# Attention in a hybrid block: values as the stationary operand, turned weights of all queries moving, weights divided before they are turned

## The chip, the cores and the metric

The kernel is one program on one core of a Trainium2 chip. The metric is the device time of one execution in microseconds, the median of several runs. TensorE (PE) multiplies matrices; its weight loads are shown as an engine of their own (PEld). VectorE (DVE) and ScalarE (ACT) do elementwise work, GpSimd (POOL) a little, and SyncE (SP) issues most of the transfers. Each engine works through its own queue in order.

## What is computed

Two layers (D 1024, 256 positions, batch 1) of a block: a modulated norm, three branches that mix the positions, and a mixture of experts. The branches are latent attention (8 heads, value width 64), an mLSTM, and dilated attention (8 heads, width 64), which the kernel folds into one masked softmax per head. Cut to what matters:

```
s = einsum('bqhd,bkhd->bhqk', q, k) * scale          # 8 heads, 256 x 256, causal mask
p = softmax(s)                                       # over the keys
o = einsum('bhqk,bkhd->bqhd', p, v)                  # value width 64
ya, yc = o of latent and of dilated attention        # 256 x 512 each
merged = g0*(ya @ w_branch_a) + g1*(yb @ w_branch_b) + g2*(yc @ w_branch_c)
x = x + g_a * (merged @ w_out);  x = x + g_f * moe(norm(x))
```

## The kernel before, in words

All data is fp32. The large products (projections, gates, branch outputs) are made by `dense` and `mm3` (lines 469 to 487): each operand is split into a rounded part and a rest, both of type fp32r, and three matmuls are added up (lines 474, 475, 476). The split of the weights is one ACT copy and one DVE subtraction for each 128x512 piece (line 365), into buffers `rs`, of which four are left for weights. `ul` and `uh` are the split input, read by every projection. DVE also does the products of the modulation (line 284), which have nothing to do with the branches.

`softmax_pv` (line 713) is called four times: for latent attention (called from line 796) and dilated attention (line 954), in each of two layers. It works on 128 queries at a time (t = 0 with 128 keys, t = 1 with 256 keys). For each head TensorE makes the scores (lines 794, 951), DVE adds the mask and takes the row maximum in one operation (line 731), a small DVE operation turns it into the bias (734, 736), and ACT takes the exponential and its row sum `den` (739). Then TensorE turns each 128x128 block of weights P (745), and ACT copies four turned heads at a time from PSUM into T (746). The product with the values (750) has the turned weights of one head as stationary operand (128 keys x 128 queries) and the 64 columns of the values as moving one; queries come out on partitions. DVE then takes the reciprocal of the sums (751) and divides the 128x512 result (752). The result is needed with its features on partitions, so `y_transposed` (756) turns it by eight TensorE transposes of 128x128 (765), and ACT and DVE split it into `yt` (768, 769), the operand of the branch's `dense`. The mLSTM branch uses `y_transposed` too, with a scale (773, 774), and goes on doing so.

An fp32 matmul of the program stands as two records in the trace: line 750 runs 24 times in a call, 96 times in four calls, and has 192 records. Transposes have one record each.

The order of the work on each engine is fixed at compile time by a scheduler that takes what is ready by its own cost model, earlier lines of the program first; so attention and dense products lie interleaved in one queue. Buffers `fs` (nine of 128x2048) are handed out first in, first out (`fs.get`, `fs.put`), so a new user of a buffer waits for its last one. Projections that follow in program order (lines 804, 808, 923, 945, 976) don't need the result of latent attention; the first that does is line 991 with b = 0. Dilated attention's result is needed by line 991 with b = 2.

Of the kernel before, what the change touches and what calls it, by code (L numbers as in the profile page):

```python
# [12 lines left out]
def _warn_once_fixed(msg, *args, **kwargs):  # L13
# [6 lines left out]
F32 = mybir.dt.float32  # L20
F32R = mybir.dt.float32r
I32 = mybir.dt.int32
AF = mybir.ActivationFunctionType
OP = mybir.AluOpType
# [14 lines left out]
C_ID, C_TRI, C_TRIS, C_MLA, C_DIL, C_MLM, C_COS, C_SIN, C_IOTA = (  # L39
    0, 128, 256, 384, 640, 896, 1024, 1088, 1152)  # L40
# [31 lines left out]
def tile_block(ctx: ExitStack, tc: tile.TileContext, x_in, c_in, cst_in, sv_in, aux_in, wada_in, ws_in, out, depth=L):  # L72
    nc = tc.nc
    PE, DVE, ACT, POOL, SP = nc.tensor, nc.vector, nc.scalar, nc.gpsimd, nc.sync
# [8 lines left out]
    def fs_tile(i, dtype=F32):  # L83
        return persist.tile([128, 2048], dtype, name=f"fs{i}")

    fs = Slots([fs_tile(i) for i in range(NB)], fs_tile)

    def xs_tile(i, dtype=F32R):
        return persist.tile([128, 2048], dtype, name=f"xs{i}")
# [4 lines left out]
    xs = Slots([xs_tile(i) for i in range(4)], xs_tile, F32R)  # L94
    rs = Slots([rs_tile(i) for i in range(NR)], rs_tile, F32R)

    def mmt(name="mm"):
        return psum.tile([128, 512], F32, name=name)

    cst = persist.tile([128, N_CST], F32, name="cst")  # L100
# [79 lines left out]
    def cut(h):  # L180
        return A0 if h < 2 else 512
# [81 lines left out]
    for hf in range(2):  # L263
        hs = slice(512 * hf, 512 * hf + 512)
        p = mmt("sm")
# [76 lines left out]
    def layer(l, tail):  # L342
# [185 lines left out]
        else:  # L528
# [21 lines left out]
            for n_, (k0, k1) in enumerate(groups):  # L550
# [11 lines left out]
                p = nxt_p  # L562
# [6 lines left out]
                for j, do in enumerate((first_chunk, second_chunk, third_chunk)):  # L569
# [3 lines left out]
                    n = cut(h_)  # L573
# [68 lines left out]
        for t in range(2):  # L642
            ts = slice(128 * t, 128 * t + 128)
# [10 lines left out]
        va = v_s[:, :1024].rearrange("p (t n) -> p t n", t=2)  # L654
# [18 lines left out]
        scq = work.tile([128, 2, 8], F32, name="scq", bufs=1)  # L673
        for t in range(2):
            ts = slice(128 * t, 128 * t + 128)
# [34 lines left out]
        fs.put(cq_s, up_s, up2_s)  # L710
        pump()

        def softmax_pv(kq, masks, scale, vv, out_s):

            for t in range(2):
                nk = 128 * (t + 1)
                per = 512 // nk
                P_s, T_s = fs.get(), fs.get()
                P = P_s[:, :8 * nk].rearrange("p (h n) -> p h n", h=8)
                T = T_s[:, :8 * nk].rearrange("p (b h n) -> p b h n", b=t + 1, h=8)  # L720
                den = work.tile([128, 8], F32, name="den")
                mx = work.tile([128, 8], F32, name="mx")
                for g in range(8 // per):
                    p = mmt("sm").rearrange("p (h n) -> p h n", h=per)
                    h0 = g % 2 + 4 * (g // 2)
                    hs = slice(h0, h0 + 2 * per - 1, 2)
                    for j in range(per):
                        kq(t, h0 + 2 * j, p[:, j])
                    for j in range(per):
                        h = h0 + 2 * j  # L730
                        DVE.tensor_tensor_reduce(p[:, j], p[:, j], masks[:, 128 * (1 - t):], 1.0, -3.0e38,
                                                 OP.add, OP.max, mx[:, h:h + 1])
                    if scale is None:
                        DVE.tensor_scalar(mx[:, hs], mx[:, hs], -1.0, None, op0=OP.mult)
                    else:
                        DVE.scalar_tensor_tensor(mx[:, hs], mx[:, hs], -1.0, scale[:, t, hs], op0=OP.mult, op1=OP.mult)
                    for j in range(per):
                        h = h0 + 2 * j
                        ACT.activation(P[:, h], p[:, j], AF.Exp, scale=1.0 if scale is None else scale[:, t, h:h + 1], bias=mx[:, h:h + 1],
                                       accum_out=den[:, h:h + 1])  # L740
                for b in range(t + 1):
                    for g in range(2):
                        p = mmt("sm").rearrange("p (h n) -> p h n", h=4)
                        for j in range(4):
                            PE.transpose(p[:, j], P[:, 4 * g + j, 128 * b:128 * b + 128], ident)
                        ACT.activation(T[:, b, 4 * g:4 * g + 4], p, AF.Copy)
                po = mmt("sm").rearrange("p (h d) -> p h d", h=8)
                for h in range(8):
                    for b in range(t + 1):
                        PE.matmul(po[:, h], T[:, b, h], vv[:, b, 64 * h:64 * h + 64], start=b == 0, stop=b == t)  # L750
                DVE.reciprocal(den, den)
                DVE.tensor_tensor(out_s[:, t].rearrange("p (h d) -> p h d", h=8), po,
                                  den[:, :, None].to_broadcast([128, 8, 64]), op=OP.mult)
                fs.put(P_s, T_s)

        def y_transposed(y, scale=None):

            yt_s = xs.get(F32R)
            yt = yt_s.rearrange("p (a b n) -> p a b n", a=2, b=4)
            for bb in range(2):  # L760
                p = mmt("sm").rearrange("p (b n) -> p b n", b=2)
                for b in range(2):
                    for t in range(2):
                        c = (2 * bb + b) * 128
                        PE.transpose(p[:, b, 128 * t:128 * t + 128], y[:, t, c:c + 128], ident)
                if scale is None:
                    s = slice(2 * bb, 2 * bb + 2)
                    ACT.activation(yt[:, 0, s], p, AF.Copy)
                    DVE.tensor_tensor(yt[:, 1, s], p, yt[:, 0, s].bitcast(F32), op=OP.subtract)
                else:  # L770
                    for b in range(2):
                        s = 2 * bb + b
                        ACT.activation(yt[:, 0, s], p[:, b], AF.Copy, scale=scale(s))
                        DVE.scalar_tensor_tensor(yt[:, 1, s], p[:, b], scale(s), yt[:, 0, s].bitcast(F32),
                                                 op0=OP.mult, op1=OP.subtract)
            return yt_s, yt

        qT_s, kT_s = fs.get(), fs.get()
# [2 lines left out]
        for t in range(2):  # L781
            ts = slice(128 * t, 128 * t + 128)
            for src, dst, g in ((qc, qT, V_GQ), (kc, kT, V_GK)):
                for gg in range(2):
                    p = mmt("sm")[:96].rearrange("p (h n) -> p h n", h=4)
# [2 lines left out]
                    o = dst[:, 4 * gg:4 * gg + 4, ts]  # L788
                    ACT.activation(o, p, AF.Copy, scale=sv[:96, g:g + 1])
        fs.put(qc_s, kc_s)  # L790
        ya_s = fs.get()
        ya = ya_s[:, :1024].rearrange("p (t n) -> p t n", t=2)
        def kq_a(t, h, p):
            PE.matmul(p, qT[:, h, 128 * t:128 * t + 128], kT[:, h, :128 * (t + 1)], start=True, stop=True)

        softmax_pv(kq_a, cst[:, C_MLA:C_MLA + 256], scq, va, ya)
        fs.put(qT_s, kT_s, v_s)
        yaT_s, yaT = y_transposed(ya)
        fs.put(ya_s)
        pump()  # L800


# [105 lines left out]
        hg = work.tile([128, 4], F32, name="hg", bufs=1)  # L908
        DVE.tensor_scalar(hg, col(V_HG, 4), 0.5, None, op0=OP.mult)
        ybT_s, ybT = y_transposed(yb, lambda s: hg[:, s:s + 1])  # L910
        fs.put(mo_s)
        pump()


        dn_s, dT_s, dv_s = fs.get(), fs.get(), fs.get()
        dn = dn_s.rearrange("p (a t n) -> p a t n", a=2, t=2)
        dT = dT_s.rearrange("p (a b n) -> p a b n", a=2, b=4)
        dv = dv_s[:, :1024].rearrange("p (t n) -> p t n", t=2)
        yc = dv_s[:, 1024:].rearrange("p (t n) -> p t n", t=2)
        dq8 = work.tile([128, 1], F32, name="dq8", bufs=1)  # L920
        POOL.tensor_scalar(dq8, col(V_DQ), 0.125, None, op0=OP.mult)
        for a in range(2):
# [13 lines left out]
            for bb in range(2):  # L936
                p = mmt("sm").rearrange("p (b n) -> p b n", b=2)
# [11 lines left out]
        def kq_c(t, h, p):  # L949
            r0 = 64 * (h % 2)  # L950
            PE.matmul(p, dT[r0:r0 + 64, 0, h // 2, 128 * t:128 * t + 128], dT[r0:r0 + 64, 1, h // 2, :128 * (t + 1)],
                      start=True, stop=True)

        softmax_pv(kq_c, cst[:, C_DIL:C_DIL + 256], None, dv, yc)
        fs.put(dT_s)
        ycT_s, ycT = y_transposed(yc)
        fs.put(dv_s)
        pump()


# [2 lines left out]
        for b, (yT_s, yT) in enumerate(((yaT_s, yaT), (ybT_s, ybT), (ycT_s, ycT))):  # L963
# [10 lines left out]
            g = g_s.rearrange("p (t n) -> p t n", t=2)  # L974
# [4 lines left out]
            if b == 1:  # L979
# [6 lines left out]
                p = mmt("sm")[:, :160]  # L986
# [21 lines left out]
        for kk, p in transposed(mg):  # L1008
            s = slice(2 * kk, 2 * kk + 2)
# [10 lines left out]
        def small(name, *shape):  # L1020
            return work.tile([128] + list(shape), F32, name=name, bufs=1)
# [219 lines left out]
        ex, d = small("ex", 2, 4), small("d", 2, 4)  # L1241
# [101 lines left out]
    for l in range(depth):  # L1343
        tail = layer(l, tail)
# [130 lines left out]
```

## Time and profile before

| what | value |
|---|---|
| runs, us | 803.78, 804.21, 800.3; median 803.78 |
| profiled execution, own time, us | 806.04 |
| its span from the first to the last instruction, us | 804.3 |
| mean granted TensorE clock | 0.975 of full |
| PE, DVE, ACT busy, share of the span | 95%, 70%, 48% |
| moved by DMA | 234.47 MB, mean 292 GB/s |

The profiled execution lies 2.3 us above the median of the runs. Busy shares are averages over stages with different limits: in the span there are two layers, each with a mixing part (about 20 to 295 us and 412 to 682 us) and an expert part, in which the transfers run near 420 GB/s. A busy TensorE means that a matmul is in its pipeline; how many it gets through is read from the start times of a row and of the row after it.

### The profile page before, as it was taken

The numbers are of one execution on the slowest core, as the hardware profiler recorded it, in microseconds if no ns is written. First come the engines' busy times: TensorE is split into PE (matmuls) and PEld (weight loads), VectorE is DVE, ScalarE is ACT, GpSimd is POOL, SyncE is SP. The second block draws the span as 40 slices with busy tenths as digits, with TensorE's granted clock in tenths as the row PEclk, the third lists the DMA queues.
The fourth block names the chain that finished last, engine by engine and source line by source line (L and its number), as shares of the span: only waits on it lengthen the run. The fifth ranks groups of instructions, "written<-read, shape, count | busy, mean of one in ns | idle before, by whom it ended". The sixth has DMA issues, their size and how long they took to land. (4 is left out here: it accounts for less than half of the span.)

```text
span 804.3 us, 12512 instructions
## 1 busy us (share of the span) xinstructions
PE 760.3 (95%) x4524; PEld 516.8 (64%) x4524; DVE 563.7 (70%) x1414; ACT 386.0 (48%) x851; POOL 30.0 (4%) x58
## 2 busy tenths in 40 slices
PE   4999999999999979999969999999999998999996
PEld 2885887878888854333349588888888876533332
DVE  6889978988899775323379998998757576633234
ACT  6467755664454533111167775576555543512111
POOL 0103000100000010000000400000000001000000
PEclk9999988999999989999989999999999999799999
DMA  8983654788989964999957367778885654499993
GB/s 338 406 343 116 250 211 157 262 309 330 384 302 426 383 247 171 423 421 420 420 211 262 114 253 261 238 262 288 330 326 201 246 202 154 167 420 421 420 422 143
DMA packets 36115, 234.47 MB, mean 292 GB/s; under 512 B 4017, under 2 KB 4689, under 8 KB 10450
## 3 DMA queue, kind: packets, MB, share of 16 engines
q1 hardware_dynamic: 35410, 231.52, 74.5%
q0 software_dynamic: 576, 2.10, 0.8%
q8 instruction: 37, 0.61, 0.3%
q14 instruction: 28, 0.23, 0.1%
q10 hardware_dynamic: 64, 0.02, 0.0%
HBM read 232.55 MB, written 1.06 MB: 290 GB/s over the span
## 5 line engine op out<-in xcount | busy, mean ns | idle before, releaser
L365 ACT ACTIVATE rs<-wa 128x512 fp32r<-128x512 f32 (+1 forms) x224 | 134.9, 633 | 90.1 <-PE mm L475 58.6
L474 PE MATMUL mm<-rs,rs 128*128 128x512 f32 (+1 forms) x432 | 172.1, 401 | 6.2 <-ACT rs L565 5.6
L365 DVE TENSOR_TENSOR rs<-wa,rs 128x512 fp32r<-128x512 f32 (+1 forms) x224 | 148.5, 683 | 39.5 <-ACT rs L365 26.7
L475 PE MATMUL mm<-rs,rs 128*128 128x512 f32 (+1 forms) x432 | 174.2, 404 | 0.4 <-DVE rs L462 0.3
L476 PE MATMUL mm<-rs,rs 128*128 128x512 f32 (+1 forms) x432 | 174.2, 404 | 0.0
L284 DVE SCALAR_TENSOR_TENSOR wa<-wa,cb 128x1024 f32<-128x1024 f32 x90 | 108.0, 1216 | 0.0
L474 PEld LDWEIGHTS mm<-rs,rs 128*128 128x128 f32 x432 | 82.2, 192 | 23.0 <-ACT rs L565 6.9
L475 PEld LDWEIGHTS mm<-rs,rs 128*128 128x128 f32 x432 | 82.7, 191 | 16.6 <-DVE rs L566 1.1
L476 PEld LDWEIGHTS mm<-rs,rs 128*128 128x128 f32 x432 | 83.1, 192 | 15.7 <-issue 1.3
L1210 DVE SCALAR_TENSOR_TENSOR th<-th,mm 128x256 f32<-128x256 f32 x16 | 6.7, 421 | 82.2 <-ACT th L1209 82.2
L1201 PE MATMUL mm<-fs,xs 128*32 128x512 f32 x384 | 58.7, 593 | 0.0
L1201 PE MATMUL mm<-wa,xs 128*32 128x512 f32 x320 | 54.0, 604 | 0.0
L1209 ACT ACTIVATE th<-mm 128x256 f32<-128x256 f32 x16 | 6.1, 383 | 95.8 <-PE mm L1201 95.8
L109 ACT ACTIVATE fs<-fs 128x512 fp32r<-128x512 f32 x32 | 20.1, 629 | 56.3 <-DVE fs L1234 56.3
L1201 PE MATMUL mm<-rs,xs 128*32 128x512 f32 x320 | 42.8, 594 | 0.0
L109 DVE TENSOR_TENSOR fs<-fs,fs 128x512 fp32r<-128x512 f32 x32 | 22.1, 692 | 22.8 <-ACT fs L109 22.8
L474 PE MATMUL mm<-rs,xs 128*128 128x512 f32 x96 | 37.6, 392 | 0.0
L476 PE MATMUL mm<-rs,xs 128*128 128x512 f32 x96 | 37.5, 391 | 0.0
L475 PE MATMUL mm<-rs,xs 128*128 128x512 f32 x96 | 37.4, 390 | 0.0
L1234 DVE TENSOR_TENSOR fs<-mm,fs 128x512 f32<-128x512 f32 x32 | 22.0, 687 | 20.9 <-PE mm L1232 20.9
L365 ACT ACTIVATE rs<-fs 128x512 fp32r<-128x512 f32 x40 | 23.8, 627 | 22.9 <-PE mm L475 14.8
L1201 PEld LDWEIGHTS mm<-fs,xs 128*32 128x32 f32 x384 | 15.9, 110 | 29.0 <-issue 28.4
(333 smaller groups left out, 1276.8 us busy)
## 6 DMA issues: line engine op xcount, KB each, us to landing
wa<-in_ws_dram SPq DMA_DIRECT2D x83, 1024.0 KB, 7.1
fs<-in_ws_dram SPq DMA_DIRECT2D x47, 1024.0 KB, 10.3
wa<-in_wada_dram SPq DMA_DIRECT2D x40, 1024.0 KB, 5.3
rs<-in_ws_dram SPq DMA_DIRECT2D x30, 1024.0 KB, 12.4
wa<-in_wada_dram SPq DMA_DIRECT2D x10, 512.0 KB, 9.9
wa<-in_ws_dram SPq DMA_DIRECT2D x6, 512.0 KB, 9.2
fs<-in_wada_dram SPq DMA_DIRECT2D x6, 512.0 KB, 10.0
fs<-row POOLq DMA_DIRECT2D x4, 512.0 KB, 7.8
```

The source lines that it names most:

```text
L109: return ACT.activation(h, src, AF.Copy), DVE.tensor_tensor(l, src, h.bitcast(F32), op=OP.subtract)
L284: DVE.scalar_tensor_tensor(w, w, 0.5, cb, op0=OP.mult, op1=OP.mult, accum_out=mods[l][:, 2 * i + j:2 * i + j + 1])
L365: pinned(ACT.activation(h[:, cs_], r[:, cs_], AF.Copy), DVE.tensor_tensor(lo[:, cs_], r[:, cs_], h[:, cs_].bitcast(F32), op=OP.subtract))
L474: PE.matmul(o, ah[:, kb + k, ts], hv[:, k], start=st, stop=False)
L475: PE.matmul(o, al[:, kb + k, ts], hv[:, k], start=False, stop=False)
L476: PE.matmul(o, ah[:, kb + k, ts], lv[:, k], start=False, stop=en)
L1201: queued(PE.matmul(pgu[64 * t + 32 * i:64 * t + 32 * i + 32], xg[kb // 2][:, kb % 2, 2 * q + i, t], wv[i][:, k], start=kb == 0, stop=kb == 7))
L1209: ACT.activation(th, pgu[:, :256], AF.Tanh, scale=0.5)
L1210: DVE.scalar_tensor_tensor(th, th, 1.0, pgu[:, :256], op0=OP.add, op1=OP.mult)
L1234: DVE.tensor_tensor(y, py[hf], rows[:, 1, hs], op=OP.mult)
```

## The change

In `softmax_pv` the weights P are divided by their sums before they are turned: for t = 0 by one DVE multiplication of 128x1024, for t = 1 by eight ACT copies of 128x256 with a scale. The reciprocal moves ahead of the turns. The turned weights of both t are kept (T0 for keys 0 to 127, all 256 queries; T1 for keys 128 to 255, the last 128 queries). Then for each head the values (128 keys x 64) are the stationary operand and the turned weights the moving one, 256 columns for T0 and 128 for T1. Two heads write the two halves of the partitions of one PSUM tile. The result has its features on partitions, so that the transposes of `y_transposed` and the division of the result fall away for the two attentions; the split into `yt` stays, now from this PSUM tile. The buffers P0, P1 and T are held from the start of a call to its end; before, two were held for each t, and one for the result.

```diff
-        def softmax_pv(kq, masks, scale, vv, out_s):
+        def softmax_pv(kq, masks, scale, vv):
+            P0_s, P1_s, T_s = fs.get(), fs.get(), fs.get()
+            T0 = T_s.rearrange("p (h n) -> p h n", h=8)
+            T1 = P0_s[:, 1024:].rearrange("p (h n) -> p h n", h=8)
             for t in range(2):
...
-                for b in range(t + 1):
-                    for g in range(2):
+                DVE.reciprocal(den, den)
+                if t == 0:
+                    DVE.tensor_tensor(P, P, den[:, :, None].to_broadcast([128, 8, nk]), op=OP.mult)
+                for g in range(2):
+                    if t:
+                        for h in range(4 * g, 4 * g + 4):
+                            ACT.activation(P[:, h], P[:, h], AF.Copy, scale=den[:, h:h + 1])
+                    for b in range(t + 1):
                         p = mmt("sm").rearrange("p (h n) -> p h n", h=4)
                         for j in range(4):
                             PE.transpose(p[:, j], P[:, 4 * g + j, 128 * b:128 * b + 128], ident)
-                        ACT.activation(T[:, b, 4 * g:4 * g + 4], p, AF.Copy)
-                po = mmt("sm").rearrange("p (h d) -> p h d", h=8)
-                for h in range(8):
-                    for b in range(t + 1):
-                        PE.matmul(po[:, h], T[:, b, h], vv[:, b, 64 * h:64 * h + 64], start=b == 0, stop=b == t)
-                DVE.reciprocal(den, den)
-                DVE.tensor_tensor(out_s[:, t].rearrange("p (h d) -> p h d", h=8), po,
-                                  den[:, :, None].to_broadcast([128, 8, 64]), op=OP.mult)
-                fs.put(P_s, T_s)
+                        ACT.activation(T1[:, 4 * g:4 * g + 4] if b else T0[:, 4 * g:4 * g + 4, ts], p, AF.Copy)
+            yt_s = xs.get(F32R)
+            yt = yt_s.rearrange("p (a b n) -> p a b n", a=2, b=4)
+            for g in range(2):
+                po = mmt("sm").rearrange("p (h n) -> p h n", h=2)
+                for hh in range(2):
+                    for b, T in enumerate((T0, T1)):
+                        for i in range(2):
+                            h = 4 * g + 2 * hh + i
+                            PE.matmul(po[64 * i:64 * i + 64, hh, 128 * b:], vv[:, b, 64 * h:64 * h + 64], T[:, h], start=b == 0, stop=b == 1,
+                                      skip_group_check=True)
+                s = slice(2 * g, 2 * g + 2)
+                ACT.activation(yt[:, 0, s], po, AF.Copy)
+                DVE.tensor_tensor(yt[:, 1, s], po, yt[:, 0, s].bitcast(F32), op=OP.subtract)
+            fs.put(P0_s, P1_s, T_s)
+            return yt_s, yt
...
-        softmax_pv(kq_a, cst[:, C_MLA:C_MLA + 256], scq, va, ya)
+        yaT_s, yaT = softmax_pv(kq_a, cst[:, C_MLA:C_MLA + 256], scq, va)
         fs.put(qT_s, kT_s, v_s)
-        yaT_s, yaT = y_transposed(ya)
-        fs.put(ya_s)
...
-        softmax_pv(kq_c, cst[:, C_DIL:C_DIL + 256], None, dv, yc)
-        fs.put(dT_s)
-        ycT_s, ycT = y_transposed(yc)
-        fs.put(dv_s)
+        ycT_s, ycT = softmax_pv(kq_c, cst[:, C_DIL:C_DIL + 256], None, dv)
+        fs.put(dT_s, dv_s)
```

`y_transposed` keeps only its branch with a scale.

## Rows read from the trace of the kernel before

**Rows 1.** Windows around three of the four calls, then layer 0's mixing and its experts' start.
```profile
core 0: us, PE busy (x) PEld busy (x) DVE busy (x) ACT busy (x) POOL busy (x), PEclk, DMA share, GB/s
84.00:110.00 26.00, 26.00 (x163) 22.11 (x163) 22.17 (x71) 17.84 (x51) 0.00 (x0) 1.00 0.73 281
148.00:175.00 27.00, 25.96 (x172) 21.45 (x171) 22.96 (x73) 19.14 (x56) 0.88 (x1) 1.00 0.85 320
536.00:565.00 29.00, 27.88 (x182) 23.27 (x181) 26.34 (x79) 20.16 (x57) 0.00 (x0) 1.00 0.81 290
60.00:260.00 200.00, 197.33 (x980) 157.96 (x979) 179.18 (x453) 118.29 (x274) 10.90 (x19) 0.97 0.73 273
300.00:320.00 20.00, 20.00 (x128) 8.48 (x129) 11.64 (x39) 9.06 (x16) 0.00 (x0) 0.93 0.42 170
```

**Rows 2.** Waits in total: engine, line, waited for: us, times, longest.
```profile
ACT rs L365 <- PE mm L475: 73.3, 52, 6.4
PEld sm L745 <- ACT fs L739: 5.6, 11, 1.6
```

**Rows 3.** Groups of instructions by line and shape: busy us, mean ns; idle before.
```profile
L750 PE MATMUL sm<-fs,fs 128*128 128x64 f32 x192 | 23.4, 270 | 0.0
L765 PE MATMUL sm<-cst,fs 128*128 128x128 f32 x48 | 8.1, 278 | 0.2 <-DVE nt L122 0.2
```

**Rows 4.** Timeline of PE, first layer: start us, length, line, records merged.
```profile
81.82 1.05 PE L787 MATMUL sm<-cst,fs 128*96 128x128 f32 x8
82.70 1.95 PE L794 MATMUL sm<-fs,fs 96*128 96x128 f32 x16
84.41 0.48 PE L474 MATMUL mm<-rs,rs 128*128 128x512 f32 x1
...
93.92 2.81 PE L794 MATMUL sm<-fs,fs 96*128 96x256 f32 x12
...
96.38 0.59 PE L475 MATMUL mm<-rs,rs 128*128 128x512 f32 x1
...
102.67 3.46 PE L750 MATMUL sm<-fs,fs 128*128 128x64 f32 x30
...
105.96 0.28 PE L765 MATMUL sm<-cst,fs 128*128 128x128 f32 x1
```

**Rows 5.** Timeline of PE where matmuls use a part of the array.
```profile
149.76 1.52 PE L951 MATMUL sm<-fs 64*128 64x128 f32 x16
...
151.22 0.50 PE L476 MATMUL mm<-rs,rs 128*128 128x512 f32 x1
...
159.12 2.10 PE L951 MATMUL sm<-fs 64*128 64x256 f32 x16
...
161.15 0.50 PE L476 MATMUL mm<-rs,rs 128*128 128x512 f32 x1
...
341.14 3.64 PE L1201 MATMUL mm<-fs,xs 128*32 128x512 f32 x32
344.60 0.59 PE L1201 MATMUL mm<-wa,xs 128*32 128x512 f32 x1
```

**Rows 6.** Groups of instructions on DVE and ACT by line and shape.
```profile
L284 DVE SCALAR_TENSOR_TENSOR wa<-wa,cb 128x1024 f32<-128x1024 f32 x90 | 108.0, 1216 | 0.0
L752 DVE TENSOR_TENSOR fs<-sm,den 128x512 f32<-128x512 f32 x8 | 5.5, 692 | 8.9 <-PE sm L750 8.9
L773 ACT ACTIVATE xs<-sm,hg 128x256 fp32r<-128x256 f32 x8 | 3.5, 472 | 4.0 <-PE sm L765 3.6 <-DVE xs L774 0.3
```

**Rows 7.** Windows around a fall of the granted clock, and the same work in layer 1.
```profile
108.00:115.00 7.00, 7.00 (x40) 5.42 (x39) 6.70 (x15) 4.68 (x11) 0.00 (x0) 1.00 0.17 69
115.00:125.00 10.00, 10.00 (x28) 6.83 (x25) 6.58 (x16) 3.18 (x7) 0.00 (x0) 0.50 0.62 210
...
500.00:506.00 6.00, 6.00 (x26) 4.38 (x27) 5.79 (x13) 3.00 (x7) 0.00 (x0) 1.00 0.64 217
```

**Rows 8.** Timeline of PE ahead of that fall.
```profile
112.44 1.97 PE L861 MATMUL sm<-fs,cst 4*128 4x256 f32 x8
```

More of the change, by code (lines that the diff above doesn't have):

```diff
@@ L717, in softmax_pv @@
                 per = 512 // nk
-                P_s, T_s = fs.get(), fs.get()
-                P = P_s[:, :8 * nk].rearrange("p (h n) -> p h n", h=8)
-                T = T_s[:, :8 * nk].rearrange("p (b h n) -> p b h n", b=t + 1, h=8)
+                P = (P1_s if t else P0_s)[:, :8 * nk].rearrange("p (h n) -> p h n", h=8)
+                ts = slice(128 * t, 128 * t + 128)
                 den = work.tile([128, 8], F32, name="den")
@@ L745, in softmax_pv, with y_transposed @@
                             PE.transpose(p[:, j], P[:, 4 * g + j, 128 * b:128 * b + 128], ident)
-                        ACT.activation(T[:, b, 4 * g:4 * g + 4], p, AF.Copy)
-                po = mmt("sm").rearrange("p (h d) -> p h d", h=8)
-                for h in range(8):
-                    for b in range(t + 1):
-                        PE.matmul(po[:, h], T[:, b, h], vv[:, b, 64 * h:64 * h + 64], start=b == 0, stop=b == t)
-                DVE.reciprocal(den, den)
-                DVE.tensor_tensor(out_s[:, t].rearrange("p (h d) -> p h d", h=8), po,
-                                  den[:, :, None].to_broadcast([128, 8, 64]), op=OP.mult)
-                fs.put(P_s, T_s)
-        def y_transposed(y, scale=None):
+                        ACT.activation(T1[:, 4 * g:4 * g + 4] if b else T0[:, 4 * g:4 * g + 4, ts], p, AF.Copy)
[14 more added lines that the diff above has]
+            return yt_s, yt
+        def y_transposed(y, scale):
             yt_s = xs.get(F32R)
@@ L765, in y_transposed @@
                         PE.transpose(p[:, b, 128 * t:128 * t + 128], y[:, t, c:c + 128], ident)
[L766 to L775, printed above, removed]
+                for b in range(2):
+                    s = 2 * bb + b
+                    ACT.activation(yt[:, 0, s], p[:, b], AF.Copy, scale=scale(s))
+                    DVE.scalar_tensor_tensor(yt[:, 1, s], p[:, b], scale(s), yt[:, 0, s].bitcast(F32),
+                                             op0=OP.mult, op1=OP.subtract)
             return yt_s, yt
@@ L790, in layer @@
         fs.put(qc_s, kc_s)
-        ya_s = fs.get()
-        ya = ya_s[:, :1024].rearrange("p (t n) -> p t n", t=2)
         def kq_a(t, h, p):
             PE.matmul(p, qT[:, h, 128 * t:128 * t + 128], kT[:, h, :128 * (t + 1)], start=True, stop=True)
-        softmax_pv(kq_a, cst[:, C_MLA:C_MLA + 256], scq, va, ya)
+        yaT_s, yaT = softmax_pv(kq_a, cst[:, C_MLA:C_MLA + 256], scq, va)
         fs.put(qT_s, kT_s, v_s)
-        yaT_s, yaT = y_transposed(ya)
-        fs.put(ya_s)
         pump()
```

## The prediction, made before the changed kernel was run

> **What bounds the kernel now.** I read the windows first. Around the calls of the attention TensorE is busy for 26.00 of 26 us, 25.96 of 27 and 27.88 of 29, at a granted clock of 1.00 [rows 1]: the two attentions lie inside dense products in one full queue. DVE is next with 22 to 26 us, ACT with 18 to 20. The waits agree: ACT's split of the weights waits 73.3 us in total for TensorE to give buffers back, while TensorE's turns wait 5.6 us for the exponentials [rows 2], and that is weight loads that start late, mostly under a running matmul. So TensorE sets the pace in the mixing, and the question is how much TensorE time the change takes out. Whether it reaches the end: as layer 0's experts start, the transfers run at a share of 0.42 [rows 1], so an earlier start is not held up by data. I count the saving in full, in both layers.
>
> Busy time and mean ns are no price on TensorE, since matmuls overlap; the price is the distance between starts in the timeline. Eight transposes take 82.70 - 81.82 = 0.88 us, 0.11 each; sixteen fp32 records of 128 columns (84.41 - 82.70)/16 = 0.107 each; twelve of 256 columns (96.38 - 93.92)/12 = 0.205; thirty of line 750, with 64 columns, (105.96 - 102.67)/30 = 0.110 [rows 4]. The last is what the reader is to see: 64 moving columns cost as much as 128, so each record there does half of what its time would allow.
>
> **Removed from TensorE.** Line 750: 192 records [rows 3] x 0.110 = 21.1 us. Line 765: 48 transposes in three branches [rows 3], of which the two attentions give up 32: x 0.11 = 3.5 us. Together 24.6 us in four calls.
>
> **Added to TensorE.** Two records for each fp32 matmul, as line 750 has. A call has 8 heads, so 16 records of 256 columns and 16 of 128: 16 x 0.205 + 16 x 0.107 = 5.0 us one after the other, 2.5 us if the two halves of the array run side by side. Two rows bear on that. 32 records of line 1201, four outputs side by side by 32 columns of the array, start within 344.60 - 341.14 = 3.46 us, 0.108 each for 512 columns, a quarter of the 0.41 that twice 0.205 gives [rows 5]. Line 951, which uses half of the array's rows, does its 16 records of 256 columns in 161.15 - 159.12 = 2.03 us; alone they would take 3.3 [rows 4, 5]. Halves side by side by columns of the array stand in no row; I take full overlap, since row and column cases both show it: 4 x 2.5 = 10.0 us. The other end is 20.0.
>
> Going into and out of a split array costs something too: 2.03 us against half of 3.3 leaves 0.4 us for a visit; the block with 128 columns leaves 1.46 - 0.86 = 0.6, some of it from records that did not find a partner [rows 5]. The eight matmuls of a group become ready together, with one ACT copy, so I take one visit for a group, two for a call: 8 x 0.4 = 3.2 us, the lower end 8 x 0.3, the upper one below.
>
> TensorE's balance: -24.6 + 10.0 + 3.2 = **-11.4 us**.
>
> The Trainium skill (TensorE: Matmul & The Clock Gate, "Measured speedup vs the span model") reports 2.38 times for three column tiles. Spread evenly that is 1.6 times for two, an estimate, so 12.6 us in place of 10.0 and a balance of -8.8. The row of line 1201 shows the full four times in this kernel, and the measurement decides.
>
> **DVE.** It gives up two divisions of 128x512 in a call, 0.69 us each, and with them 8.9 us in which it stood still behind them for line 750 [rows 6]. It gets one multiplication of 128x1024, nearest row 1.22 us [rows 6]: -0.2 us for a call. The reciprocals are the same, earlier; before and after, they wait for the last exponential, and the weight subtractions and modulation products queue behind them. The multiplication stands right behind the reciprocal, so it adds 1.2 us to what those wait, where the two divisions added more. I cost DVE at nothing; its cover is that TensorE is the fuller engine.
>
> **ACT.** Eight scaling copies of 128x256 for a call. They read SBUF and no row shows this; the nearest is 0.47 us from PSUM [rows 6]. 8 x 0.47 = 3.8 us, 15 us in all. The copies of turned weights and the split into `yt` are as many as before. ACT has 18 to 20 us of 26 to 29 in the windows, so 3.8 fit, but they delay the splits queued behind them. The splits run ahead of TensorE by four buffers, which hides a delay of that size while the buffers are full.
>
> **The chain.** Before, a turn waited for one head's exponential, and the product of t = 0 could go early. Now the turns of t = 0 wait for the reciprocal and a multiplication of all heads (1.4 us more), those of t = 1 for the reciprocal and four scalings (2.1 us more), and no product can begin before t = 1 is turned. Nobody needs the result soon; the projections and gates behind it fill TensorE. But the order is fixed at compile time, and where the scaling is slower than the scheduler thinks, TensorE stands at a turn with ready work behind it. It does so today for 5.6 us at most [rows 2]; the bounds are 5.6 gained and, with 3.5 us in each call, 14 lost. I take one scaling copy for each call, 4 x 0.4 = 1.6 us lost.
>
> Buffers: P0, P1 and T are held longer, T0 instead of two tiles. In the first-in-first-out queue the mLSTM's E comes onto what P0 leaves, and its first write comes only after the call; the first gate of b = 0 comes onto an mLSTM buffer that is free by then. No DMA is issued or moved. I cost these at nothing; if the cover goes, DVE's first write to E waits for the end of the call's products, some 2 us once for a layer.
>
> **Sum.** -11.4 + 1.6 = -9.8 us, so 806.04 becomes 796.2 for the profiled execution. That execution lies 2.3 us above the median of the runs shown; against the median 803.78 I give **794.0**.
>
> **The rivals.** About 0.5%, 4 us, is what a measurement of this kernel tells from no change.
>
> *No overlap.* If halves by columns run one after the other, the products cost 20.0 us, and -24.6 + 20.0 + 3.2 + 1.6 leaves 0.2: 804. Against it stands line 1201's row; for it, only that no row has halves of 64.
>
> *Visits cut up.* The scheduler does cut attention up with dense products (the timeline has turns and line 474 in turns). If it put a dense matmul between every two pairs of heads, a call would have 8 visits in place of 2: 24 x 0.4 = 9.6 us more, so -0.2, 803.6. The Trainium skill (TensorEngine Tiling (Array Packing), "Key Properties") says that a change of tiling mode drains the engine, and so speaks against this change; by that rule each cut would cost a drain, and the rows agree with 0.4 us for going in and out. Against the rival: line 750 ran in a run of 30 [rows 4], and all eight matmuls of a group are ready at once.
>
> *DVE takes over in layer 0.* From 60 to 260 us DVE is busy for 179 of 200 [rows 1], with the modulation products. If it leaves no room there, layer 0's half is lost: -4.9, 799. Against: much of DVE's rest is waiting that the change takes away.
>
> *The clock.* From 115 to 125 us the granted clock is 0.50, the lower of its two levels (1.2 GHz), after matmuls that used four rows of the array; the same work in layer 1 ran at 1.00 [rows 7, 8]. About 5 us are lost there. Everything moves by some us, so the fall may go (789) or come in layer 1 too (799). I see no reason for either.
>
> *ACT takes over: slower.* In each call the turns of t = 1 wait for ACT, which has the eight scalings on top of exponentials, copies and splits. If the split weights run out meanwhile, TensorE stands still for the scalings (3.8) and the reciprocal and multiplication of t = 0 (1.4): 5.2 us a call, 20.8 in all, against 11.4 saved: 803.8 + 9.4 = 813. It decides from 2.9 us a call. For it: ACT is at two thirds in the windows; against: the 73.3 us in which ACT waits for TensorE [rows 2].
>
> **How the numbers follow.** The forecast as it stands 0.50, with 790 to 798 as its own range (below: visits at 0.3, no loss and a little gain at the turns; above: visits at 0.6 and twice the loss at the turns, -24.6 + 10.0 + 4.8 + 3.2 = -6.6); the clock's fall gone 0.13; DVE 0.10; no overlap 0.10; cut up 0.08; ACT 0.09. Faster by over 0.5% (below 799.8): 0.50 + 0.13 + 0.10 = 0.73. Same: 0.10 + 0.08 = 0.18. Slower: 0.09. The range from 785 (clock's fall gone and the waits at turns gone too) to 804.5 takes in all but ACT and a little of the clock.
>
> **What would show it.** Right: the PE records fall by 192 + 32 - 128 = 96; pairs on 64 columns of the array start a few ns apart; a block of a group lasts near 1.25 + 0.4 us; no transposes of the attentions' results; windows around the calls shorter by 2 to 3 us each with TensorE still full. Wrong step by step: starts of the new matmuls 0.2 us apart without partners (overlap), dense records between them (visits), idle time of TensorE behind ACT's scalings (chain), TensorE waiting for line 365's DVE half (DVE). The prediction is wrong if TensorE's windows are no longer full, or the time is above 804.5 or below 785.

## The result, and the profile after

The changed kernel takes 792.27 us (median of four runs, 791.47 to 796.75) against 804.0 (four runs, 800.3 to 805.12): a ratio of 0.987, interval 0.9843 to 0.9898. The forecast was 794.0, faster, with 785 to 804.5 as range. The profiled execution took 792.1 us, 13.9 less than the one of before.

The page's first part after the change. Of 4524 PE records 96 are gone, as counted in the prediction; ACT has 12.6 us more.

```profile
span 790.3 us, 12341 instructions
PE 744.7 (94%) x4428; PEld 499.7 (63%) x4428; DVE 561.9 (71%) x1410; ACT 398.6 (50%) x883; POOL 28.8 (4%) x58
```

The windows that answer to [rows 1]; the columns are those of before. TensorE is as full as it was around the calls, so it still sets the pace there. DVE in layer 0 went from 179 to 187 of 200 us, ACT from 118 to 131; in the second window DVE is now the fuller one, 26.80 of 27 us against 22.96 before.

```profile
60.00:260.00 200.00, 196.92 (x977) 155.05 (x976) 186.90 (x465) 130.70 (x298) 9.28 (x19) 1.00 0.78 294
...
84.00:110.00 26.00, 26.00 (x136) 21.03 (x135) 24.75 (x75) 20.89 (x59) 0.00 (x0) 1.00 0.82 303
148.00:175.00 27.00, 25.83 (x139) 20.82 (x138) 26.80 (x80) 20.02 (x58) 0.56 (x1) 1.00 0.78 282
...
536.00:565.00 29.00, 27.83 (x155) 21.37 (x154) 24.16 (x59) 20.99 (x52) 0.00 (x0) 1.00 0.86 326
```

TensorE's timeline at the new product of the first call (line 765; line 754 are the turns). It is read from start to start: ten records in 108.84 - 107.61 = 1.23 us, then four turns of the other heads in the middle of the group, six records in 0.79, two dense matmuls, sixteen records in 1.45. Three visits to the split array, where the prediction had two; the other three calls have the same 10, 6 and 16 records.

```profile
107.20 0.48 PE L474 MATMUL mm<-rs,rs 128*128 128x512 f32 x1
107.61 1.30 PE L765 MATMUL sm<-fs,fs 128*64 128x256 f32 x10
108.84 0.66 PE L754 MATMUL sm<-cst,fs 128*128 128x128 f32 x4
109.43 0.86 PE L765 MATMUL sm<-fs,fs 128*64 128x256 f32 x6
110.22 0.50 PE L475 MATMUL mm<-rs,rs 128*128 128x512 f32 x1
110.56 0.40 PE L476 MATMUL mm<-rs,rs 128*128 128x512 f32 x1
110.88 1.52 PE L765 MATMUL sm<-fs,fs 128*64 128x256 f32 x16
112.33 0.39 PE L844 MATMUL sm<-smx,cst 128*128 128x4 f32 x2
```

The new operations among the groups by line and shape: the scaling copies (750) took 0.52 us each and the multiplication (746) 1.22.

```profile
L750 ACT ACTIVATE fs<-fs,den 128x256 f32<-128x256 f32 x32 | 13.7, 522 | 0.0
...
L746 DVE TENSOR_TENSOR fs<-fs,den 128x1024 f32<-128x1024 f32 x4 | 4.9, 1222 | 0.0
```

And the waits that answer to [rows 2]: ACT still waits 53.1 us for TensorE (73.3 before); the turns now wait for the scalings, weight loads 5.1 us and matmuls 2.3. Before, they waited for the exponentials, weight loads 5.6 us and matmuls 2.2 (the last line below is of the kernel before).

```profile
ACT rs L365 <- PE mm L475: 53.1, 45, 6.4
...
PEld sm L754 <- ACT fs L750: 5.1, 7, 1.6
...
PE sm L754 <- ACT fs L750: 2.3, 2, 1.2
```

```profile
PE sm L745 <- ACT fs L739: 2.2, 2, 1.1
```

**TensorE's time by kind of work.** Busy time can't be added on this engine, so I took the distance from each matmul record's start to the next one's, put it down to the first record's line, and counted stretches at the lower clock by half. Sums in us over the whole execution:

| kernel | product | turns of weights | turns of results, all branches | scores | these four | dense | everything |
|---|---|---|---|---|---|---|---|
| before | 20.6 | 7.7 | 4.4 | 17.1 | 49.86 | 403.1 | 776.1 |
| changed | 13.9 | 10.2 | 1.6 | 16.9 | 42.62 | 402.0 | 767.6 |
| unsplit | 21.1 | 9.8 | 1.5 | 16.9 | 49.22 | 399.7 | 771.5 |
| one_visit | 11.0 | 9.8 | 1.6 | 16.9 | 39.34 | 402.0 | 764.8 |
| halves_apart | 14.3 | 9.5 | 1.7 | 16.9 | 42.35 | 400.3 | 767.5 |
| cut_up, its transposes with the product | 23.0 | 10.2 | 1.5 | 17.1 | 51.81 | 400.3 | 775.5 |
| scaling_alone | 20.5 | 9.2 | 4.4 | 17.0 | 51.03 | 401.0 | 776.6 |
| no_scaling | 11.0 | 9.5 | 1.5 | 19.5 | 41.44 | 399.8 | 764.5 |

The dense column has the same 1632 records in every kernel and differs by 3 us between profiles, also between two profiles of one kernel (402.0 and 398.9 for one_visit); that is the noise of the last column. The turns of weights rose without more waiting. A turn ahead of a dense matmul is charged 0.03 to 0.05 us, one ahead of another turn 0.11 to 0.12, and in the changed kernel 71 of the 96 stand ahead of another turn, before 50; part of the rise is time that stood with the dense matmuls before.

The expert matmuls of line 1201 (1207 after the change) divide the span into stages. With the lower clock counted by half, the changed kernel takes 4.4 us less to the first of them in layer 0 (5.6 less in a second profile), and 4.3 less (3.8) from the last of layer 0 to the first of layer 1; from the first to the last of layer 0 it takes 93.9 us against 93.8. So both layers give their half and the experts take nothing back.

**The clock.** The profiled execution of before had a stretch at the lower clock from 115 to 125 us [rows 7]; the profiled one of the changed kernel has none there. A second profile of the changed kernel has it, ten us long, at the same place in the program: the fall belongs to neither kernel. First the changed kernel, then the same kernel again; the column before the last two is the granted clock.

```profile
115.00:125.00 10.00, 10.00 (x50) 7.28 (x49) 9.17 (x24) 6.58 (x16) 0.00 (x0) 1.00 0.44 165
```

```profile
108.00:119.00 11.00, 11.00 (x70) 8.06 (x68) 9.28 (x23) 7.57 (x16) 0.00 (x0) 1.00 0.66 254
120.00:129.50 9.50, 9.50 (x23) 6.42 (x22) 6.41 (x14) 4.50 (x9) 0.00 (x0) 0.50 0.25 99
```

So a comparison of two profiles holds some 5 us of chance. Each execution comes with its mean clock, 0.968 to 0.983 over 40 of the kernel before (for example 808.67 us at 0.968 and 800.0 at 0.983), 0.973 to 0.981 over nine of the changed kernel. A straight line through all 103 executions of these kernels, with one slope, gives 0.57 us for each 0.001 of mean clock. With it, at the same clock and against the kernel before (twice the standard error of the fit):

| kernel | us against before at the same clock |
|---|---|
| scaling_alone | -0.7 +- 0.7 |
| cut_up | -2.0 +- 0.7 |
| unsplit | -3.1 +- 0.7 |
| changed | -9.1 +- 0.7 |
| halves_apart | -9.8 +- 1.1 |
| no_scaling | -12.1 +- 0.9 |
| one_visit | -13.7 +- 0.7 |

Set beside the column "these four", each kernel's time lies some 2 to 4 us lower against the kernel before than its attention work on TensorE does: the changed kernel -7.2 in the column and -9.1 in time, scaling_alone +1.2 and -0.7. Where these 2 to 4 us come from is not shown. Against scaling_alone, which divides early too, column and time agree for the changed kernel: -8.4 and -8.5.

### The profile page after: what moved, and what is told of

Read it like the earlier page. It is cut to its first block, busy times and chain, and to the rows that moved or that the text cites. A ratio compares the mean times of both kernels' runs of the same rounds, so it can differ in the third digit from the quotient of the medians.

```text
span 790.3 us, 12341 instructions
## 1 busy us (share of the span) xinstructions
PE 744.7 (94%) x4428; PEld 499.7 (63%) x4428; DVE 561.9 (71%) x1410; ACT 398.6 (50%) x883; POOL 28.8 (4%) x58
## 3 DMA queue, kind: packets, MB, share of 16 engines
HBM read 232.55 MB, written 1.06 MB: 296 GB/s over the span
## 5 line engine op out<-in xcount | busy, mean ns | idle before, releaser
L474 PE MATMUL mm<-rs,rs 128*128 128x512 f32 (+1 forms) x432 | 170.5, 397 | 6.7 <-ACT rs L565 5.7
L475 PE MATMUL mm<-rs,rs 128*128 128x512 f32 (+1 forms) x432 | 171.6, 398 | 0.5 <-DVE rs L462 0.3
L476 PE MATMUL mm<-rs,rs 128*128 128x512 f32 (+1 forms) x432 | 171.6, 398 | 0.0
```

Source lines behind the costliest of these rows:

```text
L474: PE.matmul(o, ah[:, kb + k, ts], hv[:, k], start=st, stop=False)
L475: PE.matmul(o, al[:, kb + k, ts], hv[:, k], start=False, stop=False)
L476: PE.matmul(o, ah[:, kb + k, ts], lv[:, k], start=False, stop=en)
```

## The experiments

**changed_again.** No edit.

> The changed kernel once more, as the yardstick for the others and to see the granted clock beside each time. Theory (TensorE sets the pace; about 8 to 10 us of the 12 are TensorE work taken out, the rest is a fall of the granted clock in layer 0 that mostly no longer comes): executions at a mean clock near 0.981 lie near 792, those near 0.977 about 4 us higher. Rival (the whole gain is work and the clock is chance on both sides): times do not go with the clock.

Measured: 794.35 us (793.34 to 795.35), ratio 0.9878, interval 0.9852 to 0.9904. Its five executions go with the clock, from 793.34 at 0.979 to 795.35 at 0.973, and so do those of the first set, three at 0.981 near 792 and one at 0.977 at 796.75. The first reading of 792.27 lies 2.1 us below this one. Its median clock was 0.981 against 0.978 here, worth 1.7 us on the line above: that much was luck. The 4 us that the theory gave for 0.004 of clock are 2.3 on the line, and the fall in layer 0 is there in this profile, so that it mostly goes with the change is not borne out.

**unsplit: no two heads side by side.**

```diff
-PE.matmul(po[64 * i:64 * i + 64, hh, 128 * b:], vv[:, b, 64 * h:64 * h + 64], T[:, h], ...)
+PE.matmul(po[i][:, hh, 128 * b:], vv[:, b, 64 * (h - i):64 * (h - i) + 128], T[:, h], ...)
...
+for i in range(2):
+    r = slice(64 * i, 64 * i + 64)
+    ACT.activation(yt[r, 0, s], po[i][r], AF.Copy)
+    DVE.tensor_tensor(yt[r, 1, s], po[i][r], yt[r, 0, s].bitcast(F32), op=OP.subtract)
```

> The product with the array unsplit: for each head the values of both heads of its pair (128 columns) are stationary, so that the matmuls come out on all partitions and no two run side by side; each head's half is then read from a PSUM tile of its own, so the split into yt is made in two halves of the partitions. Theory: TensorE's product takes 5.0 us a call instead of about 3.8, and no going in and out of a split array: 1.2 to 2.5 us a call, 5 to 8 us slower than the changed kernel, about 798. Rival (TensorE's work in the product is not what counts): as fast as the changed kernel.

Measured: 798.84 us (796.22 to 806.83, 12 runs), ratio 0.9948, interval 0.9921 to 0.9975; at the same clock 6.0 us slower than the changed kernel. The product takes 21.1 us in place of 13.9. Its timeline in the first call: the last 26 of 32 records take 112.00 - 107.85 = 4.15 us, one after the other.

```profile
107.85 4.32 PE L765 MATMUL sm<-fs,fs 128*128 128x128 f32 x26
112.00 0.28 PE L846 MATMUL sm<-smx,cst 128*128 128x4 f32 x2
```

What follows: without the split array the product costs what it did before (20.6); making the values stationary gains nothing by itself. Two thirds of the gain, 6.0 of 9.1 us, are the heads side by side. What is left, 3.1 us, is not explained: the turns of the results are 2.9 us less than before, but the turns of the weights are 2.0 us more, and the four columns together fell by only 0.6. The two more splits into `yt` in each group went into this kernel too. They are on ACT and DVE and their share wasn't separated; the product's 7.2 us over the changed kernel are enough for the whole difference.

**one_visit: no turns inside a group's products.**

```diff
+turn = PE.transpose(p[:, j], P[:, 4 * g + j, 128 * b:128 * b + 128], ident)
...
+behind_of(PE.matmul(po[64 * i:64 * i + 64, hh, 128 * b:], ...), turn)
```

> The products of both groups are put behind the last turn on TensorE, so that no turns fall into the middle of a group's products. Theory (TensorE's work and its goings in and out of the split array count): one visit of three is saved, and the records that ran without a partner find one, 0.5 to 0.7 us a call, 2 to 3 us faster than the changed kernel, about 790. Rival (the order is worth nothing, or the product comes later and something waits): the same as the changed kernel or slower.

Measured: 789.19 us (785.88 to 791.42), ratio 0.9809, interval 0.978 to 0.9838. All 32 records now stand in one block in each call, 111.08 - 108.33 = 2.75 us. One visit of three is left, so two were saved, where the expectation has one.

```profile
108.01 0.38 PE L754 MATMUL sm<-cst,fs 128*128 128x128 f32 x2
108.33 2.82 PE L765 MATMUL sm<-fs,fs 128*64 128x256 f32 x32
111.08 0.39 PE L844 MATMUL sm<-smx,cst 128*128 128x4 f32 x2
```

> The products behind the last turn once more, on the chip of this call. Theory (3 us of TensorE time fewer in the product): 2 to 5 us faster than the changed kernel at the same clock, a ratio to the kernel before near 0.981. Rival (the first reading was chance): a ratio near 0.988.

Measured on another chip: 788.37 us (786.84 to 793.28), ratio 0.9818, interval 0.9781 to 0.9854. Both readings together are 4.6 us below the changed kernel at the same clock. That is more than the 2 to 3 of the first expectation; TensorE's product explains 2.9 of it, and the rest is not explained. This version beats both kernels.

**no_scaling: what the early division costs.** The reciprocal, the multiplication and the scaling copies are taken out.

> Leaves out the division by the sums: no reciprocal, no multiplication of t = 0, no scaling copies of t = 1; the attention is not normalised. Theory (the scaling is hidden behind dense products except for some waits at the turns): 0 to 3 us faster than the changed kernel, 789 to 792. Rival (the scalings on ACT and the longer chain give back a good part of the gain): 5 us or more faster, below 787.

Measured: 792.28 us (789.56 to 792.7), ratio 0.9851, interval 0.9825 to 0.9877; 3.0 us below the changed kernel at the same clock, the edge of what the theory gave. But the order of TensorE's work changed too. The scheduler put the 32 records of a call into one block by itself (the product takes 11.0 us, as in one_visit), and it cut up the scores of dilated attention: their last 16 records in the first layer take 1.06 us for four and 1.92 for twelve, where [rows 5] has 2.03 for all. The scores cost 2.6 us more than in the changed kernel.

```profile
96.75 2.82 PE L759 MATMUL sm<-fs,fs 128*64 128x256 f32 x32
99.50 0.38 PE L838 MATMUL sm<-smx,cst 128*128 128x4 f32 x2
...
144.77 1.13 PE L953 MATMUL sm<-fs 64*128 64x256 f32 x4
145.83 0.44 PE L748 MATMUL sm<-cst,fs 128*128 128x128 f32 x2
```

So this kernel alone doesn't give the price of the scaling. What stands is that one_visit, which keeps the scaling and has the same product, is no slower than this kernel: by that the scaling's 13.7 us of ACT and 4.9 us of DVE are hidden, but for about 1 us if the dearer scores here count in full (12.1 + 2.6 against 13.7, an estimate).

**scaling_alone: the early division on the kernel before.**

```diff
+DVE.reciprocal(den, den)
+if t == 0:
+    DVE.tensor_tensor(P, P, den[:, :, None].to_broadcast([128, 8, nk]), op=OP.mult)
...
+            ACT.activation(P[:, h], P[:, h], AF.Copy, scale=den[:, h:h + 1])
...
-DVE.reciprocal(den, den)
-DVE.tensor_tensor(out_s[:, t].rearrange("p (h d) -> p h d", h=8), po, den[:, :, None].to_broadcast([128, 8, 64]), op=OP.mult)
+ACT.activation(out_s[:, t].rearrange("p (h d) -> p h d", h=8), po, AF.Copy)
```

> The kernel before with the early division alone: reciprocal, multiplication and scaling copies ahead of the turns, the product as before (turned weights stationary, queries on partitions, results turned by eight transposes), and ACT copies the result out of PSUM in place of DVE's division, so that DVE no longer stands still behind the product. Theory (the gain is TensorE work taken out by the product and the turns of the result): no gain, 0 to 4 us slower than the kernel before at the same clock, since the turns wait longer. Rival (the gain comes from DVE, which no longer waits 8.9 us for the product): 4 to 9 us faster than the kernel before.

Measured: 801.91 us (799.38 to 803.87, 12 runs), ratio 0.9973, interval 0.9946 to 0.9999; at the same clock -0.7 +- 0.7. The DVE rival (4 to 9 us) falls: DVE's waits behind the product are gone here, ACT now waits 7.6 us in its place, and nearly nothing comes of it. The theory's "0 to 4 slower" was also a little off, to the other side.

```profile
L756 PE MATMUL sm<-fs,fs 128*128 128x64 f32 x192 | 25.2, 270 | 0.2
...
L757 ACT ACTIVATE fs<-sm 128x512 f32<-128x512 f32 x8 | 4.8, 597 | 7.6 <-PE sm L756 7.6
```

**cut_up: what a visit costs.** On top of one_visit, the order fixed and one transpose behind every pair:

```diff
+dm = mmt("sm")
...
+o = PE.transpose(dm[:, :128], ident, ident)
+behind_of(o, turn)
```

> Products behind the last turn, with one transpose of the whole array (128x128, nobody reads it) put behind every pair of heads' matmuls of a block of keys: eight visits to the split array in each call in place of one. Theory (a visit costs 0.3 to 0.4 us): 32 x 0.11 for the transposes and 28 x 0.3 to 0.4 for the visits, 12 to 15 us slower than one visit, 801 to 804. Rival (going in and out costs nothing beside the transposes): 3.5 us slower, 793.

Measured: 800.41 us (797.27 to 802.56, 10 runs), ratio 0.9964, interval 0.994 to 0.9989; at the same clock 11.7 us slower than one_visit. In the first call the 32 records and 8 transposes take 113.50 - 107.70 = 5.80 us in place of 2.75; without 8 x 0.11 for the transposes, seven more visits cost 2.17 us, 0.31 each. The time fell just short of the 12 to 15 us that the theory gave.

```profile
107.70 0.65 PE L766 MATMUL sm<-fs,fs 128*64 128x256 f32 x4
108.29 0.33 PE L770 MATMUL sm<-cst 128*128 128x128 f32 x1
108.55 0.44 PE L766 MATMUL sm<-fs,fs 128*64 128x128 f32 x4
...
113.33 0.33 PE L770 MATMUL sm<-cst 128*128 128x128 f32 x1
113.50 0.28 PE L850 MATMUL sm<-smx,cst 128*128 128x4 f32 x2
```

So the rival "visits cut up" had the right mechanism at too high a price, 0.31 us in place of 0.4. Cut up like this, the change is worth 2 us, of which the 32 transposes themselves take about 3.5; eight visits alone would have left some 5.5, an estimate from these figures.

**halves_apart: does the queue's order matter.** On top of one_visit, each matmul put behind the one before it:

```diff
-for hh in range(2):
-    for b, T in enumerate((T0, T1)):
-        for i in range(2):
+for i in range(2):
+    for hh in range(2):
+        for b, T in enumerate((T0, T1)):
...
+            turn = o
```

> Products behind the last turn, and in each group first the four matmuls of the one half of the array's columns, then the four of the other, in that fixed order. Theory (TensorE takes its queue in order, so only neighbours run side by side): the product takes about twice as long, 20 us in four calls in place of 11, so 8 to 9 us slower than with the halves in turns, about 798. Rival (TensorE looks ahead past matmuls of a busy half): as fast as with the halves in turns, about 789.

Measured: 791.45 us (790.84 to 794.72, 4 runs), ratio 0.9861, interval 0.9819 to 0.9904; 3.9 us slower than one_visit at the same clock, between the two expectations. The block of a call takes 111.23 - 107.66 = 3.57 us in place of 2.75, not twice as long.

```profile
107.66 3.63 PE L765 MATMUL sm<-fs,fs 128*64 128x256 f32 x32
111.23 0.39 PE L846 MATMUL sm<-smx,cst 128*128 128x4 f32 x2
```

Start by start, the first four records (one head of the first half) run alone, 0.267, 0.216, 0.109 and 0.109 us apart; the next head's first record of this half and the first record of the other half then start 0.006 us apart, though three records of the first half stand between them in the queue. (The trace doesn't name the half; records of one half start 0.109 us or more apart here, so a record 0.006 us behind another is of the other half.) From there on two run side by side, until four are left alone at the end. Neither theory was right: TensorE starts matmuls of a free half past waiting ones of a busy half, but only a few of them.

## Why the prediction was right, point by point

- **The bound.** TensorE's sums fell by 8.5 us, 7.2 of them in the attention's columns and the rest within the noise, and the time at the same clock by 9.1 +- 0.7. Over the kernels both go the same way, from cut_up to one_visit. That the saving is counted in full, in both layers, was right.
- **Removed, 24.6 us.** The starts give 20.6 for the product and 2.9 for the results' turns, 23.5 in all.
- **Added, 10.0 for the records.** In one_visit the two records of a pair start 0.006 to 0.007 us apart, and the next pair follows after 0.216 us for 256 columns and 0.109 for 128, so that the records take 2.60 of a block's 2.75 us, 10.4 in four calls. Unsplit, single records are as far apart as these pairs. Full overlap of the two column halves was right; unsplit shows what its absence costs.
- **Visits, 3.2 us.** This is the term that was mis-sized. There were three a call, not two, because turns of the other heads fell into the first group, and the cut left some records without a partner. In the changed kernel the product takes 13.9, so 13.9 - 10.4 = 3.5 us stand inside its blocks. A visit puts about 0.15 us inside a block (2.75 - 2.60) and the rest of its 0.31 on the matmuls beside it: twelve visits are 3.7 us, 1.8 of them inside, and the lost partners are the other 1.7. Together that is about 5.4 us, an estimate, in place of 3.2. The price of 0.4 a visit was high (0.31 in cut_up), the number low, and lost partners weren't priced at all.
- **The chain, 1.6 us lost.** The turns' share of TensorE's time rose by 2.5 us, but 2.3 us of its matmuls standing still behind the scalings stand in place of 2.2 behind the exponentials: the wait that this term prices didn't grow. scaling_alone doesn't show a loss in the time either (-0.7), and no_scaling gains nothing that one_visit lacks. So a loss here is not shown; that it is small is.
- **Sum.** -9.8 predicted, -9.1 at the same clock. The sum came out this near in part by luck: the attention's columns give -7.2, and the other 2 us are the unexplained ones. The measured 792.27 is lower than 794.0 by the clock, which was luck too.
- **DVE and ACT at nothing.** no_scaling against one_visit bears this out for the scaling. DVE rose to 187 of 200 us in layer 0 without becoming the bound: layer 0 gave 4.4 us, as much as layer 1. From 148 to 175 us, though, it has next to nothing to spare.
- **The rivals.** No overlap: unsplit takes the overlap out; it came out at 798.84 rather than 804. Of these 5 us, 3.2 are visits that I had charged it and that an unsplit array doesn't make. Cut up: it is real at 0.31 us a visit, but the scheduler cut less. DVE in layer 0: the two layers' equal shares speak against it. The clock: the fall went in one profile and stayed in the other, as chance would have it. ACT taking over: it does not happen; ACT still waits 53.1 us for TensorE.

The Trainium skill (TensorEngine Tiling (Array Packing), "Key Properties") has a drain at each change of tiling mode. By that rule each visit costs, and cut_up agrees, with 0.31 us a visit.

## What to carry to other kernels

Where TensorE's queue is full, price matmuls by the distance of their starts: an fp32 record with 64 moving columns cost as much as one with 128, so making the narrow operand the stationary one and putting two heads side by side took the product from 20.6 to 11.0 us at best. The swap without the second head beside it left it at 21.1. Keep such a block in one piece, with the halves in turns; each cut costs about 0.3 us and may leave matmuls without a partner. And put each execution's granted clock beside its time before two profiles are compared.

## What the runs showed of the hardware

- Two 64-column halves of the array ran fully side by side in fp32: 32 records in 2.75 us (one_visit), against about 0.16 us a record unsplit, 5 us for 32.
- Matmuls of a free half started ahead of waiting ones of a busy half, past three records in halves_apart. So the opening's statement that each engine works through its queue in order doesn't hold for TensorE there. The Trainium skill (TensorE: Matmul & The Clock Gate, "The mechanism") says that matmuls keep to strict queue order; for two column halves the starts in this run differ, and the measurement decides.
- The same program had its granted clock at the lower level for ten us at one place in one execution and not in another. Over 40 executions of the kernel before, times from 799.65 to 809.63 us went with mean clocks from 0.983 to 0.968.
